# Gate weight sums kept in DRAM, head 0's data and the first token sums loaded from an earlier place, and the pools of branch A moved, in a hybrid attention encoder block

## The chip, the cores and the metric

One Trainium2 chip, of which the kernel uses one core. The metric is the device time of one execution in microseconds (us), lower is better. The engines are called as the profile calls them: PE (TensorE matmuls) with PEld (its weight loads), DVE (VectorE), ACT (ScalarE), POOL (GpSimd) and SP (SyncE, which issues every DMA of this kernel from one queue, in order).

## The reference

One encoder block on 1024 tokens of width 1024, in float32, with 16 meta tokens in front. Two attention branches share one input projection; each branch is projected back to width 1024, multiplied by a sigmoid gate, and the two are added; then comes an output projection and a SwiGLU feed-forward part.

```python
proj = h @ w_in                       # qa, ka, va, qb, kb, vb, ga, gb
y_a = differential_attention(qa, ka, va, ...)   # 4 heads, two softmax maps each, all keys
y_b = windowed_gqa(qb, kb, vb, sink)            # 8 heads, 128-wide window
merged = sigmoid(ga) * (y_a @ w_ba) + sigmoid(gb) * (y_b @ w_bb)
h = h + merged @ w_o
h = h + (silu(n(h) @ w_gate) * (n(h) @ w_up)) @ w_down
return rms_norm(h)[:, 16:]
```

In differential attention a head's weights are `softmax(s1) - lambda * softmax(s2)`; each score matrix is one "map" m of the kernel.

## The kernel before

**Precision.** Every large matrix product is made of three float32r products: an operand is split into a high half (a copy by ACT, line 114) and a low half (a subtraction, line 115, on POOL or DVE), and high x high, high x low and low x high are added in PSUM. `split` is this helper, so a split operand costs one ACT and one POOL or DVE instruction whatever line calls it.

**Stages.** Input norm and transposition; projections, with branch B's attention (`units_b`) run between those of branch A's heads (`project_a`, lines 561 to 573); then branch A's attention, into whose PE order the gate products are woven (lines 823 to 866); then the merge (lines 901 to 974), the output projection, and the feed-forward part. Projected queries, keys and values of branch A go to DRAM (`qa_d`, `ka_d`, `va_d`) and come back a head at a time by `load_a(h)` (line 704).

**The gates** are two 1024 x 1024 products, made with a Strassen-like scheme of 7 products instead of 8 for each of 8 column blocks k: 56 products (p, k) in the order `order_g` (lines 603 to 609), each of 4 steps of 3 matmuls (`gate_steps`, line 667), together 672 matmuls with 512 columns. Product 2, 1 and 4 use a block of `w_in` as it is. Products 5, 3, 6 and 7 need sums of blocks: a21+a22 (s1), s1-a11 (s2), a12-s2 (s4), a11-a21 (s3). `g_prep` (line 622) loads the raw blocks of w_in (`gr`), makes the sums in place on POOL (lines 644 to 650, four for each k, 32 in all), and splits the operand (`gop`). For products 5 and 3 it makes s1, s2 and s4 and puts s2 away in DRAM (`s2_d`); for product 1 it loads the raw blocks again. It runs three products ahead of PE. The other operand is the transposed normed input hT or a token sum; `load_sums` (line 596) overwrites parts of hT with token sums from DRAM when their readers are done. A finished product goes to DRAM (`g_d`), and products 1, 6 and 7 add what lies there (`gk`).

**Branch A's loop** (lines 831 to 859) runs over 4 heads x 8 query tiles, one tile at a time. PE's order is written out by hand: SLOTS is a string with one letter for each action of a tile, s for a chunk of scores (6 for a tile), g for one gate step, t for a transposition of the tile before, n for a step of the values and their norm. At the first tile of a head come G_FIRST (head 0) or G_HEAD gate steps; 36 steps are held back for the end. A tile's chain is: scores on PE, bias and minimum on DVE (line 737), exponential on ACT (742), scaling of map 1 on POOL (745), combination on DVE (748), a copy of the last 16 columns on POOL (749), transposes on PE (760), splits into `at` on ACT and DVE (763, 764), values on PE (773).

**What sets the order.** PE's order in branch A is manual. All other orders, and PE's order among the projections, come from a scheduler that places instructions by a simulated timeline when the kernel is built; on the chip each engine and SP's queue then run theirs strictly in order. Pools are stacks from the left and from the right of the on-chip memory: a pool opened after another was closed takes its addresses, and the first write to a tile waits for the last use of what lay there. In before, `bpool` (left, branch B's tiles) stays open until after the projections; then `gpool` (right) and `apool` (left) are opened.

Of the kernel before, what the change touches and what calls it, by code (L numbers as in the profile page):

```python
# [19 lines left out]
P = 128  # L20
# [19 lines left out]
SLOTS = "sgsgsngsgsstntnt"  # L40
S_BUFS = (2, 2)
AT_BUFS = 2
G_BUFS = 3
GV_BUFS = 4
# [4 lines left out]
G_FIRST = 30  # L49
# [21 lines left out]
def encoder_block(ctx: ExitStack, tc: tile.TileContext, x, meta, norm_mix, w_in, lq1, lk1, lq2, lk2,  # L71
# [30 lines left out]
    s2_d = [dram.tile([P, 4, P], F32, name=f"s2_d{k}") for k in range(8)]  # L102
# [124 lines left out]
    def project_v(col, name, evac):  # L227
        vt = bpool.tile([P, L + NM], F32, tag="vt", name=f"vt_{name}", bufs=1)
        project(col, K_CHUNKS, name, lambda ps, at, n: nc.scalar.copy(vt[:, at:at + n], ps))
        nc.vector.tensor_copy(vt[:, L:L + NM], vt[:, S:L])  # L230

        def turn():
            for b in range(3):
                nb = 4 if b < 2 else 1
                kp = P if b < 2 else 2 * NM
                pt = pp_bank(f"pv_{name}_{b}").rearrange("p (c t) -> p c t", c=4)
                for i in range(nb):
                    k = 4 * b + i
                    nc.tensor.transpose(pt[:kp, i, :], vt[:, k * P:k * P + kp], ident)
                evac(pt[:kp, :nb, :], 4 * b, nb, kp)  # L240
                yield

        turning_v[:] = [turn()]
# [6 lines left out]

    bpool, close_bpool = pool("bpool")
# [121 lines left out]
    def norm_x(t):  # L373
        parts = P if t < NT else NM
        i = len(done)
        done.append(t)
        tag, bufs = ("vt", 1) if i % 3 == 2 else ("bs", 2)
        xns[t] = normed(bpool, xts.pop(t)[:parts], parts, gmix, f"a{t}", tag=tag, bufs=bufs)
# [182 lines left out]
    units_b(0, qb, first_b)  # L561
# [9 lines left out]
    project_a(2)  # L571
    project_a(3)
    flush_v()
    close_bpool()
    close_psum1()


    def branch_w(p, o, src, nme, raw=None):
        w = (raw_tile(f"wbr{nme}_{o}")[:, 0:512] if raw is None else raw).rearrange("p (c n) -> p c n", n=P)
        nc.sync.dma_start(w, src[:, o * P:(o + 1) * P].rearrange("(c p) n -> p c n", p=P))  # L580
        wh = p.tile([P, 2, 4, P], F32R, tag="wh", name=f"wbh{nme}_{o}", bufs=WB_BUFS)
        split(wh[:, 0], wh[:, 1], w, nc.gpsimd)
        return wh

    def branch_mm(ps, w, src, tk):
        for j in range(4):
            for n, (a, b) in enumerate(((0, 0), (0, 1), (1, 0))):
                nc.tensor.matmul(ps, w[:, a, j, :], src(j, b, tk),  # L588
                                 start=(j == 0 and n == 0), stop=(j == 3 and n == 2))

    close_tpool()
    close_stage()
    close_wpool()
    gpool, close_gpool = pool("gpool", "right")
# [5 lines left out]
    load_sums(5, 0, 1)  # L600
# [11 lines left out]
    def g_cols(k):  # L612
        return (C_GB, C_GA)[k // 4] + k % 4 * 256

    def g_tile(name):
        return gpool.tile([P, 512], F32, tag="gv", name=name, bufs=GV_BUFS)

# [4 lines left out]
    def g_prep(n):  # L622
        p, k = order_g[n]
        at, tt = g_cols(k), nc.gpsimd.tensor_tensor

        def load(out, kh, c0, cn):
            nc.sync.dma_start(out, w_in[kh * 512:kh * 512 + 512, at + c0:at + c0 + cn].rearrange("(c p) n -> p c n", p=P))

        if p == 2:
            src = g_tile(f"g12_{k}").rearrange("p (c n) -> p c n", n=P)  # L630
            load(src, 1, 0, P)
        else:
            if p in (5, 1):
                raw = g_raw[k] = gpool.tile([P, 2, 4, 256], F32, tag="gr", name=f"gr{p}_{k}", bufs=2)
                load(raw[:, 0], 0, 0, 256)
                if p == 5:
                    load(raw[:, 1], 1, 0, 256)
                else:
                    nc.sync.dma_start(raw[:, 1, :, 0:P], s2_d[k])
                    load(raw[:, 1, :, P:256], 1, P, P)  # L640
            raw = g_raw[k]
            a11, a21, a12, a22 = (raw[:, i, :, j * P:j * P + P] for i in range(2) for j in range(2))
            if p == 5:
                tt(a21, a21, a22, ALU.add)
            elif p == 3:
                tt(a11, a21, a11, ALU.subtract)
                nc.sync.dma_start(s2_d[k], a11)
                tt(a12, a12, a11, ALU.subtract)
            elif p == 7:
                tt(a21, a11, a21, ALU.subtract)  # L650
            src = {5: a21, 3: a12, 1: a11, 6: a12, 7: a21, 4: a22}[p]
            if p in (1, 6, 7):
                kept = g_kept[p, k] = g_tile(f"gk{p}_{k}")
                nc.sync.dma_start(kept, g_place(p, k))
        op = g_ready[p, k] = gpool.tile([P, 2, 4, P], F32R, tag="gop", name=f"gop{p}_{k}", bufs=4)
        split(op[:, 0], op[:, 1], src, nc.gpsimd)

    g_prepped = [0]

    def g_ahead(n):  # L660
        while g_prepped[0] < min(n, len(order_g)):
            g_prep(g_prepped[0])
            g_prepped[0] += 1

    g_ahead(3)

    def gate_steps():
        for n, (p, k) in enumerate(order_g):
            g_ahead(n + 3)
            op, act = g_ready.pop((p, k)), G_ACT[p]  # L670
            if p in (2, 5, 1):
                g_bank[k] = pp_bank(f"pg{p}_{k}")
            ps = g_bank[k]
            for c in range(4):
                for i, (a, b) in enumerate(((0, 0), (0, 1), (1, 0))):
                    nc.tensor.matmul(ps, op[:, a, c], quad(b, *act)[:, c], start=(p in (2, 5, 1) and c == 0 and i == 0),  # L676
                                     stop=(p in (2, 3, 4) and c == 3 and i == 2), skip_group_check=True)
                if c == 3:
                    if p in (1, 6, 7):
                        st = g_kept.pop((p, k))  # L680
                        nc.vector.tensor_tensor(st, ps, st, ALU.add)
                    else:
                        st = gpool.tile([P, 512], F32, tag="g", name="gate_stage", bufs=G_BUFS)
                        nc.scalar.copy(st, ps)
                    nc.sync.dma_start(g_place(p, k), st)
                    if k == 7 and p in (2, 5, 3):
                        load_sums({2: 6, 5: 7, 3: 4}[p], *act)
                yield

    apool, close_apool = pool("apool")  # L690
    psum2, close_psum2 = pool("psum2", space=PSUM)
    psum1 = psum2
# [27 lines left out]

    def scores_a(h, t, ld, s):
# [6 lines left out]
        for m in (1, 0):  # L728
            s[m] = s0s[t % 2] if m == 0 else apool.tile([P, L], F32, tag="s1", name=f"as1_{nm}", bufs=S_BUFS[1])
# [19 lines left out]
        nc.gpsimd.tensor_copy(s[0][:, L:L + 2 * NM].rearrange("p (a k) -> p a k", a=2),  # L749
# [27 lines left out]
    def normed_a(h, c, py):  # L777
        nm = f"{h}_{c}"
        ysq = apool.tile([P, 512], F32, tag="ysq", name=f"ysq_{nm}", bufs=1)
        nc.scalar.activation(ysq, py, AF.Square)  # L780
        yg = apool.tile([P, 512], F32, tag="yg", name=f"yg_{nm}", bufs=2)
        nc.scalar.activation(yg, py, AF.Copy, scale=gsub)
        yield
        pst = bank(psum2, "sc", f"apst_{nm}", SC)
        for i in range(4):
            nc.tensor.matmul(pst[:, i:i + 1], ysq[:, i * P:(i + 1) * P], ones, start=True, stop=True)
        f = small.tile([P, 4], F32, tag="af", name=f"af_{nm}", bufs=2)
        nc.vector.tensor_scalar(f, pst[:, 0:4], 1.0 / P, EPS, ALU.mult, ALU.add)
        nc.gpsimd.tensor_tensor(f, f, neg_half, ALU.pow)
        for _ in range(N_WAIT):  # L790
            yield
        pf = bank(psum2, "sc", f"apf_{nm}", SC)
        for i in range(4):
            nc.tensor.transpose(pf[:, i * P:(i + 1) * P], f[:, i:i + 1].broadcast_to([P, P]), ident)
# [36 lines left out]
    for n in range(AH * NT + T_LAG):  # L831
        scoring, turning = iter(()), iter(())
        if n < AH * NT:
            h, t = divmod(n, NT)
            if t == 0:
                ld = load_a(h)
                fill(G_HEAD if h else G_FIRST)
            if t % 2 == 0:
                at_ = apool.tile([P, 9, 2, 256], F32R, tag="at", name=f"at{h}_{t}", bufs=AT_BUFS)
# [5 lines left out]
        for what in SLOTS:  # L845
# [18 lines left out]
    order_pe.__exit__(None, None, None)  # L864
    close_apool()
    fill(1000)
# [570 lines left out]
```

## Time and profile before

| What | us |
|---|---|
| median of 3 runs | 1504.69 |
| the three runs | 1504.47, 1504.69, 1507.2 |
| the profiled execution | 1502.53 |
| its span in the profile | 1500.8 |

The stages lie in the profile about like this (from the chain of waits and the stretches):

| Stage | from, to (us from the span's start) |
|---|---|
| input norm, projections, branch B | 0 to 307 |
| branch A with the gate products | 307 to 665 |
| merge | 674 to 763 |
| output projection | 763 to 888 |
| feed-forward and output | 888 to 1501 |

Times are us unless marked ns. A row of stretches gives start:end, length, busy time and number of instructions of each engine, the clock that PE was granted as a share of full speed, the mean busy share of the 16 DMA engines, and GB/s. In rows of groups the pair after the bar is busy time and mean ns of one. In rows of waits come the total, the number of times and the longest. "a<-b" is the tile written and the tile read, and L with a number the line of the kernel.

### The profile page before, as it was taken

The numbers are of one execution on the slowest core, as the hardware profiler recorded it, in microseconds if no ns is written. First come the engines' busy times: TensorE is split into PE (matmuls) and PEld (weight loads), VectorE is DVE, ScalarE is ACT, GpSimd is POOL, SyncE is SP. The second block draws the span as 40 slices with busy tenths as digits, with TensorE's granted clock in tenths as the row PEclk, the third lists the DMA queues.
The fourth block names the chain that finished last, engine by engine and source line by source line (L and its number), as shares of the span: only waits on it lengthen the run. The fifth ranks groups of instructions, "written<-read, shape, count | busy, mean of one in ns | idle before, by whom it ended". The sixth has DMA issues, their size and how long they took to land.

```text
span 1500.8 us, 21142 instructions
## 1 busy us (share of the span) xinstructions
PE 1434.8 (96%) x7279; PEld 1227.3 (82%) x7279; DVE 884.2 (59%) x1578; ACT 680.3 (45%) x1293; POOL 674.6 (45%) x622
## 2 busy tenths in 40 slices
PE   8999999947999999979999999999999999999997
PEld 7998989936888898868888878888888888788886
DVE  7477436503867797823440786655555554778666
ACT  6366436513655465534521563433333333344444
POOL 4599233318646454423732476554544453000344
PEclk9999999978999999989999999999999999999999
DMA  8467442297386836466740345333333333864443
GB/s 239 98 188 234 127 114 83 62 276 224 105 283 218 258 123 199 133 226 180 212 161 21 135 119 161 106 106 105 106 105 106 106 105 105 288 238 133 128 125 140
DMA packets 184570, 231.92 MB, mean 155 GB/s; under 512 B 17984, under 2 KB 115712, under 8 KB 184464
## 3 DMA queue, kind: packets, MB, share of 16 engines
q1 hardware_dynamic: 184464, 230.58, 49.2%
q8 instruction: 57, 0.93, 0.3%
q14 instruction: 49, 0.40, 0.1%
HBM read 153.26 MB, written 70.71 MB: 149 GB/s over the span
## 4 chain that ended last, share of the span: by engine, by line
PE 68%; DMA 10%; POOL 9%; issue 5%; DVE 5%; ACT 2%; SPq 1%; POOLq 0%; DVEq 0%; ACTq 0%
PE pg L1218 26%; PE pd L1312 8%; PE po L995 5%; PE pg L676 5%; PE ppa L588 4%; DMA gr<-in_w_in_dram 4%; PE pp_qb L201 3%; POOL oa L115 3%; PE aps L734 2%; PE pp_va L201 2%; DMA ak<-ka_d 2%; PE pp_qa L201 2%; PE apy L773 2%; PE pp_ka L201 2%; PE bpt L339 1%
## 5 line engine op out<-in xcount | busy, mean ns | idle before, releaser
L115 POOL TENSOR_TENSOR wop<-wf,wop 128x512 fp32r<-128x512 f32 x128 | 172.5, 1352 | 166.3 <-ACT wop L114 150.3
L1218 PE MATMUL pg<-t,wop 128*128 128x512 f32 x1056 | 242.6, 389 | 0.0
L1218 PEld LDWEIGHTS pg<-t,wop 128*128 128x128 f32 x1056 | 198.3, 188 | 41.1
L1312 PE MATMUL pd<-ob,oa 128*128 128x512 f32 x924 | 210.2, 389 | 1.8 <-DVE ob L115 1.4
L1312 PEld LDWEIGHTS pd<-ob,oa 128*128 128x128 f32 x924 | 173.3, 188 | 38.6 <-DVE ob L115 1.8
L676 PE MATMUL pg<-hT_hi,gop 128*128 128x512 f32 x448 | 168.7, 408 | 20.8 <-ACT gop L114 19.6
L1218 PE MATMUL pg<-b,wop 128*128 128x512 f32 x792 | 185.6, 392 | 2.9 <-DVE c L1227 2.9
L1218 PEld LDWEIGHTS pg<-b,wop 128*128 128x128 f32 x792 | 149.5, 189 | 34.8 <-issue 2.4
L115 POOL TENSOR_TENSOR oa<-ra,oa 128x512 fp32r<-128x512 f32 x33 | 44.0, 1335 | 171.8 <-ACT oa L114 170.4
L676 PEld LDWEIGHTS pg<-hT_hi,gop 128*128 128x128 f32 x448 | 87.0, 195 | 38.1 <-ACT gop L114 20.8
L114 ACT ACTIVATE wop<-wf 128x512 fp32r<-128x512 f32 x128 | 80.2, 631 | 83.7 <-PE pg L1218 48.5
L114 ACT ACTIVATE oa<-ra 128x512 fp32r<-128x512 f32 x77 | 48.6, 632 | 107.6 <-PE pd L1312 48.9
L734 PE MATMUL aps<-ak,aq 128*128 128x392 f32 (+1 forms) x384 | 91.2, 332 | 3.8 <-DVE amn L737 2.2
L742 ACT ACTIVATE as<-as,amn 128x1040 f32<-128x1040 f32 x64 | 74.5, 1164 | 43.4 <-DVE amn L737 39.6
L676 PE MATMUL pg<-hT_lo,gop 128*128 128x512 f32 x224 | 90.8, 405 | 0.0
L1053 DVE TENSOR_TENSOR s<-wf,wf 128x512 f32<-128x512 f32 x22 | 27.0, 1228 | 104.5 <-DMA wf<-in_w_ff_gate_dram 56.6
L995 PE MATMUL po<-woh,mT 128*128 128x512 f32 x384 | 88.0, 390 | 0.0
L115 POOL TENSOR_TENSOR gop<-gr,gop 128x512 fp32r<-128x512 f32 x48 | 66.9, 1396 | 41.0 <-ACT gop L114 37.9
L734 PEld LDWEIGHTS aps<-ak,aq 128*128 128x128 f32 x384 | 70.9, 192 | 17.6 <-DVE amn L737 3.5
L995 PEld LDWEIGHTS po<-woh,mT 128*128 128x128 f32 x384 | 71.9, 188 | 14.8
L737 DVE CUSTOM_DVE_ANT_0 as<-aps,dist,far_a 128x392 f32<-128x392 f32 x64 | 39.5, 618 | 62.8 <-PE aps L734 62.4
L326 POOL TENSOR_SCALAR bs<-bs,bdn 128x432 f32<-128x432 f32 (+1 forms) x64 | 39.4, 634 | 60.6 <-DVE bdn L324 52.5
(275 smaller groups left out, 3075.1 us busy)
## 6 DMA issues: line engine op xcount, KB each, us to landing
ra<-aop SPq DMA_DIRECT2D x77, 256.0 KB, 2.7
gr<-in_w_in_dram SPq DMA_DIRECT2D x24, 512.0 KB, 5.7
wf<-in_w_ff_gate_dram SPq DMA_DIRECT2D x24, 512.0 KB, 3.8
wf<-in_w_ff_up_dram SPq DMA_DIRECT2D x24, 512.0 KB, 3.8
aop<-as SPq DMA_DIRECT2D x44, 256.0 KB, 2.1
w_c<-in_w_in_dram SPq DMA_DIRECT2D x17, 512.0 KB, 5.0
aop<-c SPq DMA_DIRECT2D x33, 256.0 KB, 2.0
ts_d<-to SPq DMA_DIRECT2D x16, 512.0 KB, 3.8
```

Of the source, the lines that this page charges most:

```text
L114: nc.scalar.activation(hi, src, AF.Copy)
L115: lo_eng.tensor_tensor(lo, src, f32(hi), ALU.subtract)
L201: nc.tensor.matmul(ps[:, :n], a[:, c, :], b[:, c, at:at + n], start=(c == 0 and i == 0), stop=(c == DC - 1 and i == 2))
L326: nc.gpsimd.tensor_scalar(st[:, r, :W], st[:, r, :W], dn[:, r:r + 1], 1.0, ALU.mult, ALU.mult)
L588: nc.tensor.matmul(ps, w[:, a, j, :], src(j, b, tk), start=(j == 0 and n == 0), stop=(j == 3 and n == 2))
L676: nc.tensor.matmul(ps, op[:, a, c], quad(b, *act)[:, c], start=(p in (2, 5, 1) and c == 0 and i == 0), stop=(p in (2, 3, 4) and c == 3 and ...
L734: nc.tensor.matmul(ps[:, :n], qs[m][:, t * P:(t + 1) * P], ks[m][:, vv, k0:k0 + n], start=(vv == 0), stop=(vv == 1))
L737: nc.vector.tensor_tensor_reduce(s[m][:, k0:k0 + n], ps[:, :n], far_by, slope, low, ALU.add, ALU.min, mn[:, m, i:i + 1])
L742: nc.scalar.activation(s[m][:, 0:L], s[m][:, 0:L], AF.Exp, bias=low, scale=-1.0, accum_out=dn[:, m:m + 1])
L995: nc.tensor.matmul(ps, mT[:, c, a, t * P:(t + 1) * P], wos[q, c][:, b], start=(c == 0 and n == 0), stop=(c == DC - 1 and n == 2))
L1218: nc.tensor.matmul(ps, op[:, x, c, :], b[:, y, c, :], start=(p in (1, 2, 5) and c == 0 and n == 0), stop=(p in (4, 2, 3) and c == 3 and n ...
L1312: nc.tensor.matmul(ps[u], oa[:, a, u * P:(u + 1) * P], ob[:, b, :], start=(p in (1, 2, 5) and j == 0 and k == 0), stop=(p in (2, 3, 4) and ...
```

## The change

- `bpool` is closed as soon as branch B's second group has been written down in the program, before `project_a(2)`. `apool` is opened there, with head 0's tiles, the two score buffers of map 0 and the masked distances, and `load_a(0)` is called there. The transposed values (`vt`) get a pool of their own (`vtpool`), since `project_a` still needs them.
- A new pool `wspool` is opened next, and `weight_sums` makes the 32 sums with POOL from raw blocks `gw` (16 loads of 512 KB, 2 buffers), k = 0 to 3 after `project_a(2)` and k = 4 to 7 after `project_a(3)`, and stores them in DRAM (`ws_d`, 32 stores of 256 KB, 6 buffers). `s2_d` is gone.
- Each gate product then loads just its own operand of 256 KB (`g_load`, up to 5 products ahead) and splits it (`g_split`, up to 3 ahead). The first two operands are loaded into and split in the weight buffers of the projections (`w_g`, `w_gop`). `load_sums(5, 0, 1)` stands before `flush_v()`.
- `gpool` has smaller and other buffers (6 of 2 KB for loads, 4 of 4 KB, 3 of 2 KB, 2 of 2 KB). The map 1 scores, `at`, `ysq` and `yg` move into a pool `apool2`, opened after `wspool` is closed.
- The copy of line 749 goes from POOL to DVE.
- G_FIRST goes from 30 to 4, and SLOTS has five gate steps a tile for the first 24 tiles (SLOTS_LAST, with four as before, for the last 8).

```diff
-SLOTS = "sgsgsngsgsstntnt"
+SLOTS = "sgsgsngsgsgstntnt"
+SLOTS_LAST = "sgsgsngsgsstntnt"
...
-G_BUFS = 3
-GV_BUFS = 4
+G_BUFS = 2
+GK_BUFS = 3
+GR_BUFS = 6
+GO_BUFS = 4
...
-G_FIRST = 30
+G_FIRST = 4
...
+    def weight_sums(k, p):
+        tt = nc.gpsimd.tensor_tensor
+        raw = p.tile([P, 2, 4, 256], F32, tag="raw", name=f"gw_{k}", bufs=2)
+        for kh in range(2):
+            nc.sync.dma_start(raw[:, kh], g_weights(k, kh, 0, 256))
+        a11, a21, a12, a22 = (raw[:, i, :, j * P:j * P + P] for i in range(2) for j in range(2))
+        s1, s2, s3, s4 = (p.tile([P, 4, P], F32, tag="sum", name=f"gs{i}_{k}", bufs=6) for i in range(4))
+        tt(s1, a21, a22, ALU.add)
+        tt(s2, s1, a11, ALU.subtract)
+        tt(s4, a12, s2, ALU.subtract)
+        tt(s3, a11, a21, ALU.subtract)
+        for i, t in ((5, s1), (3, s4), (6, s2), (7, s3)):
+            nc.sync.dma_start(ws_d[i, k], t)
...
+    def g_load(n, raw=None):
+        p, k = order_g[n]
+        if raw is None:
+            raw = gpool.tile([P, 512], F32, tag="gr", name=f"gr{p}_{k}", bufs=GR_BUFS)
+        raw = raw.rearrange("p (c n) -> p c n", n=P)
+        nc.sync.dma_start(raw, ws_d[p, k] if (p, k) in ws_d else g_weights(k, *{2: (1, 0), 1: (0, 0), 4: (1, P)}[p], P))
+        g_raw[p, k] = raw
+
+    def g_split(n, op=None):
+        p, k = order_g[n]
+        if op is None:
+            op = gpool.tile([P, 2, 4, P], F32R, tag="gop", name=f"gop{p}_{k}", bufs=GO_BUFS)
+        split(op[:, 0], op[:, 1], g_raw.pop((p, k)), nc.gpsimd)
+        g_ready[p, k] = op
+        if p in (1, 6, 7):
+            kept = g_kept[p, k] = gpool.tile([P, 512], F32, tag="gk", name=f"gk{p}_{k}", bufs=GK_BUFS)
+            nc.sync.dma_start(kept, g_place(p, k))
...
     units_b(1, qb)
+    close_bpool()
+    apool, close_apool = pool("apool")
...
+    ld = load_a(0)
+    wspool, close_wspool = pool("wspool")
     project_a(2)
+    for k in range(4):
+        weight_sums(k, wspool)
     project_a(3)
+    for k in range(4, 8):
+        weight_sums(k, wspool)
+    for n in range(2):
+        g_load(n, wpool.tile([P, DC, P], F32, tag="w", name=f"w_g{n}", bufs=2)[:, 0:4].rearrange("p c n -> p (c n)"))
+        g_split(n, wpool.tile([P, DC, P], F32R, tag=("wh", "wl")[n], name=f"w_gop{n}", bufs=W_BUFS)
+                .rearrange("p (a c) n -> p a c n", a=2))
+    g_done[:] = [2, 2]
+    load_sums(5, 0, 1)
     flush_v()
-    close_bpool()
     close_psum1()
+    close_wspool()
...
+    gpool, close_gpool = pool("gpool", "right")
+    g_ahead(0)
+    psum2, close_psum2 = pool("psum2", space=PSUM)
+    psum1 = psum2
+    apool2, close_apool2 = pool("apool2")
...
-            s[m] = s0s[t % 2] if m == 0 else apool.tile([P, L], F32, tag="s1", name=f"as1_{nm}", bufs=S_BUFS[1])
+            s[m] = s0s[t % 2] if m == 0 else apool2.tile([P, L], F32, tag="s1", name=f"as1_{nm}", bufs=S_BUFS[1])
...
-        nc.gpsimd.tensor_copy(s[0][:, L:L + 2 * NM].rearrange("p (a k) -> p a k", a=2),
+        nc.vector.tensor_copy(s[0][:, L:L + 2 * NM].rearrange("p (a k) -> p a k", a=2),
...
-                ld = load_a(h)
+                if h:
+                    ld = load_a(h)
...
-        for what in SLOTS:
+        for what in SLOTS if n < 3 * NT else SLOTS_LAST:
```

More of the change, by code (lines that the diff above doesn't have):

```diff
@@ L101, in encoder_block @@
     ts_d = {p: dram.tile([P, 2, 4, 512], F32, name=f"ts_d{p}") for p in (5, 6, 7, 4)}
-    s2_d = [dram.tile([P, 4, P], F32, name=f"s2_d{k}") for k in range(8)]
+    ws_d = {(p, k): dram.tile([P, 4, P], F32, name=f"ws_d{p}_{k}") for p in (5, 3, 6, 7) for k in range(8)}
     ya_d = [dram.tile([P, S], F32, name=f"ya_d{h}") for h in range(4)]
@@ L559, in units_b, with load_sums @@
             p()
+    def load_sums(p, kh, half):
+        for hl in range(2):
+            nc.sync.dma_start(f32(quad(hl, kh, half)), ts_d[p][:, hl])
+    G_ACT = {2: (1, 0), 5: (0, 1), 3: (1, 1), 1: (0, 0), 6: (1, 0), 7: (0, 1), 4: (1, 1)}
+    G_OUT = {2: (0, 0), 5: (1, 1), 3: (0, 1), 1: (0, 0), 6: (0, 1), 7: (1, 1), 4: (1, 0)}
+    order_g = [(2, k) for k in range(4)]
+    for k in range(0, 8, 2):
+        order_g += [(p, k + i) for p in (5, 3) for i in range(2)]
+        if k < 4:
+            order_g += [(2, k + 4 + i) for i in range(2)]
@@ new lines, in g_place @@
+    def g_place(p, k):
+        row, half = G_OUT[p]
+        return g_d[2 * k + row][:, half * 512:half * 512 + 512]
+    def g_load(n, raw=None):
[14 more added lines that the diff above has]
+            nc.sync.dma_start(kept, g_place(p, k))
@@ L561, in encoder_block, with g_ahead @@
+    g_done = [0, 0]
+    def g_ahead(n):
+        for i, (what, far) in enumerate(((g_load, GR_BUFS - 1), (g_split, GO_BUFS - 1))):
+            while g_done[i] < min(n + far, len(order_g)):
+                what(g_done[i])
+                g_done[i] += 1
     units_b(0, qb, first_b)
@@ L585, in branch_mm @@
[L585 to L594, printed above, removed]
-    def load_sums(p, kh, half):
-        for hl in range(2):
-            nc.sync.dma_start(f32(quad(hl, kh, half)), ts_d[p][:, hl])
@@ L610, in encoder_block @@
-    g_ready, g_raw, g_kept, g_bank = {}, {}, {}, {}
[L612 to L616, printed above, removed]
-    def g_place(p, k):
-        row, half = G_OUT[p]
-        return g_d[2 * k + row][:, half * 512:half * 512 + 512]
[L622 to L688, printed above, removed]
@@ new lines, in branch_mm, with gate_steps @@
+    def branch_mm(ps, w, src, tk):
+        for j in range(4):
+            for n, (a, b) in enumerate(((0, 0), (0, 1), (1, 0))):
+                nc.tensor.matmul(ps, w[:, a, j, :], src(j, b, tk),
+                                 start=(j == 0 and n == 0), stop=(j == 3 and n == 2))
+    def gate_steps():
+        for n, (p, k) in enumerate(order_g):
+            g_ahead(n + 1)
+            op, act = g_ready.pop((p, k)), G_ACT[p]
+            if p in (2, 5, 1):
+                g_bank[k] = pp_bank(f"pg{p}_{k}")
+            ps = g_bank[k]
+            for c in range(4):
+                for i, (a, b) in enumerate(((0, 0), (0, 1), (1, 0))):
+                    nc.tensor.matmul(ps, op[:, a, c], quad(b, *act)[:, c], start=(p in (2, 5, 1) and c == 0 and i == 0),
+                                     stop=(p in (2, 3, 4) and c == 3 and i == 2), skip_group_check=True)
+                if c == 3:
+                    if p in (1, 6, 7):
+                        st = g_kept.pop((p, k))
+                        nc.vector.tensor_tensor(st, ps, st, ALU.add)
+                    else:
+                        st = gpool.tile([P, 512], F32, tag="g", name="gate_stage", bufs=G_BUFS)
+                        nc.scalar.copy(st, ps)
+                    nc.sync.dma_start(g_place(p, k), st)
+                    if k == 7 and p in (2, 5, 3):
+                        load_sums({2: 6, 5: 7, 3: 4}[p], *act)
+                yield
```

56 lines of the change are left out of this document (28 added, 28 removed).

## The prediction

> **What bounds the kernel now.** I read the page first, then the busy time by stretch, TensorE's waits, and the chain of waits at both ends of branch A.
>
> ```profile
> PE 1434.8 (96%) x7279; PEld 1227.3 (82%) x7279; DVE 884.2 (59%) x1578; ACT 680.3 (45%) x1293; POOL 674.6 (45%) x622
> ...
> 306.74:673.54 366.80, 320.51 (x1842) 282.81 (x1841) 225.10 (x619) 182.85 (x340) 177.23 (x165) 0.94 0.64 202
> 306.74:322.30 15.56, 0.00 (x1) 0.00 (x1) 0.56 (x1) 1.12 (x2) 0.00 (x0) 0.56 0.96 259
> 322.30:354.30 32.00, 26.74 (x90) 19.47 (x91) 0.00 (x0) 9.02 (x16) 19.05 (x16) 0.84 0.99 290
> 417.70:490.00 72.30, 67.60 (x405) 60.93 (x403) 51.24 (x147) 41.05 (x80) 38.77 (x36) 0.95 0.79 256
> 490.00:664.90 174.90, 170.85 (x1035) 153.11 (x1033) 123.87 (x338) 90.14 (x168) 77.01 (x77) 1.00 0.56 177
> 664.90:673.54 8.64, 0.20 (x2) 0.00 (x1) 1.18 (x2) 6.22 (x10) 0.00 (x0) 0.63 1.05 405
> ```
>
> Columns: stretch and length, then busy time of PE, PEld, DVE, ACT, POOL, granted clock, DMA share, GB/s. TensorE is the bound of the whole kernel, and the change touches only what lies between the last projection (306.74) and the first merge product (673.54). In these 366.80 us PE is busy 320.51; the idle time sits at the two ends and in the first heads, while from 490 to 664.9 PE is idle only 4.05 of 174.90 us (2.3%).
>
> ```profile
> PE pg L676 <- ACT gop L114: 19.6, 3, 15.6
> PE apt L760 <- DVE as L748: 8.8, 4, 4.5
> PE ppa L588 <- ACT yb L114: 8.4, 1, 8.4
> PE apt L760 <- POOL as L749: 4.3, 2, 2.7
> ...
> 306.81 5.25 DMA hT_hi<-ts_d
> ...
> 316.17 9.61 DMA ak<-ka_d
> 325.80 12.77 DMA gr<-in_w_in_dram
> ...
> 642.03 0.82 PE apy L773 x7
> 642.86 4.21 PE pg L676 x18
> 647.06 0.78 PE apst L786 x8
> ...
> 654.22 0.44 PE apf L794 x4
> ...
> 660.66 7.05 DMA tb<-yb_d
> 667.77 5.05 DMA g_d<-gate_stage
> ```
>
> The first lines are PE's waits (total, times, longest), the others the chain (start, length). The first gate product waits 15.6 us because its weights queue behind head 0's keys. The chain also gives the rate of full work: 4.21/18 = 0.234 us a gate matmul, 0.82/7 = 0.117 a value matmul, 0.44/4 = 0.11 a transpose, 0.78/8 = 0.098 for L786. A score matmul comes from PE's timeline:
>
> ```profile
> 354.31 0.51 PE L734 MATMUL aps<-ak,aq 128*128 128x392 f32 x2
> 354.65 0.39 PE L676 MATMUL pg<-hT_hi,gop 128*128 128x512 f32 x1
> ...
> 356.39 0.40 PE L734 MATMUL aps<-ak,aq 128*128 128x256 f32 x2
> 356.63 0.40 PE L676 MATMUL pg<-hT_hi,gop 128*128 128x512 f32 x1
> ```
>
> From start to start two take 0.34 us (392 wide) or 0.24 (256 wide), so a tile's scores (two maps of 2 + 2 + 2) take 2 x (0.34 + 0.34 + 0.24) = 1.84. How often each occurs, by stretch for L676 (gates), L734 (scores, 32 tiles), L760 (transposes), L773 (values), L786 and L794, with busy time and count:
>
> ```profile
> 306.74:673.54 366.80, 186.59 (x672) 0.94 0.64 202
> 306.74:673.54 366.80, 91.22 (x384) 0.94 0.64 202
> 306.74:673.54 366.80, 46.15 (x288) 0.94 0.64 202
> 306.74:673.54 366.80, 58.06 (x400) 0.94 0.64 202
> 306.74:673.54 366.80, 7.60 (x64) 0.94 0.64 202
> 306.74:673.54 366.80, 4.80 (x32) 0.94 0.64 202
> ```
>
> At the full rates that is 157.2 + 58.9 + 31.7 + 46.8 + 6.3 + 3.5 = 304.4 us of work: 62.4 of the 366.8 are lost to waits and a lowered clock, and that is all there is to win.
>
> **The change part by part.** The order in which the changed program's instructions stand on each engine decides it, and it is not what the words say. The new pool of the weight sums takes addresses of branch B's pool (its transposes and exponentials), and branch B's second group runs among the last projections until the end. So on SP the first load of a weight sum stands behind the last key store and head 0's whole load; on POOL all 32 sums stand behind branch B's last scaling, and **ahead of the first scaling of a head-0 tile** (L745). PE's order is written out: 4 gate steps, tile 0's scores, 5 steps, tile 1's scores with 5 steps, then tile 0's transposes. Those need L748's result, which needs L745's, which stands behind the last sum. PE therefore stops after 14 steps (42 matmuls) and two tiles: 42 x 0.234 + 2 x 1.84 = 13.5 us of work. (It pauses once before, as the third gate product's low half stands on POOL behind the first five sums; that lies inside the longer wait.)
>
> *When the last sum is done.* It is a matter of bytes in one queue. From head 0's load to the last weight load SP issues: head 0, 4152 KB (queries 2 x 512, keys 2 x 1040, values 1024, and 24); 16 weight loads of 512; 24 stores of sums of 256; 10 gate-weight loads of 256; 4 gate moves of 256. Sum 22,072 KB = 22.6 MB.
>
> ```profile
> 311.06 0.60 SPq L710 DMA_DIRECT2D aq<-qa_d  x1
> ...
> gr<-in_w_in_dram SPq DMA_DIRECT2D x24, 512.0 KB, 5.7
> ...
> L646 POOL TENSOR_TENSOR gr<-gr 128x512 f32<-128x512 f32 x8 | 10.3, 1285 | 0.3
> ...
> L745 POOL TENSOR_SCALAR as<-as,adn,neglam 128x1040 f32<-128x1040 f32 x32 | 38.9, 1215 | 36.4 <-DVE adn L743 33.7 <-DVE af L788 2.7
> ...
> L749 POOL COPY as<-as 128x32 f32<-128x32 f32 x32 | 7.7, 240 | 30.5 <-DVE as L748 30.5
> ...
> L748 DVE SCALAR_TENSOR_TENSOR as<-as,adn,as x32: 1280/1301/2446, 365.9 to 632.1; 128x1040 f32<-128x1040 f32 x32
> ```
>
> Head 0's load issues at 311.06 as now (SP's order ahead of it is nearly the same), and the queue is free at 312.1 (306.81 + 5.25). A full queue moved 290 GB/s (share 0.99), at best 256/0.79 = 324, at worst 259/0.96 = 270. At 290 the bytes take 78 us, to 390; the last four sums add 4 x 1.285 = 5.1: **395**. At 324: 387; at 270: 401. I take 290, whose stretch has the same mix of loads. The Trainium skill's "DMA: Bandwidth & Descriptors", Specifications, puts the HBM limit of one core at about 358 GB/s; by that the bytes would need 63 us, an estimate, and the last sum would end at 380, 15 us earlier in the sum; the row of 290 GB/s at share 0.99 doesn't reach it, though other stretches come nearer.
>
> POOL's own floor: the first pair of weights can land at 328 (5.3 MB at 324 GB/s from 312), then 32 sums and 4 gate splits of the same shape make 36 x 1.285 = 46.3: 375. Above, if loads become a chain: only two raw buffers, so each load is issued after the sums two before it; with a landing of 12.8 us as in the full queue at 325.80, a weight takes (12.8 + 5.1)/2 = 9 us, and six from about 350 end near 404, plus 5: 409.
>
> After the last sum come L745 (1.2) and L748 (1.3 alone, up to 2.4; I take 2.3, POOL being busy beside it): PE resumes at 395 + 3.5 = **398.5**, with 304.4 - 13.5 = 290.9 us still to do.
>
> *Restart.* After the 15.6 us gap:
>
> ```profile
> 322.30 0.79 PE L676 MATMUL pg<-hT_hi,gop 128*128 128x512 f32 x1 [15.56 <-ACT gop L114]
> ...
> 326.14 0.64 PE L676 MATMUL pg<-hT_hi,gop 128*128 128x512 f32 x2
> ```
>
> Eight matmuls took 3.84 us instead of 1.9, so a cold start costs 2; I take 3, since tile 1's chain is late too (bounds 2 and 5). The Trainium skill's "TensorE: Matmul & The Clock Gate", Part 1, says half clock for about 3.4 us after an idle window; that would be 1.7 us lost, an estimate, and the sum 1 us less; the 3.84 us row agrees roughly.
>
> *The rest of branch A.* Nothing else is on POOL's path there: 32 sums are gone from it, and L749 (one 128x32 copy a tile) is DVE's. Its price on DVE is not shown; between 0 and 32 x 0.24 = 7.7 us, hidden, as DVE is busy 123.87 of 174.90 us. Of the 4.3 + 8.8 us that PE waited for L749 and L748 some part returns. The fifth gate slot for 24 tiles replaces the first fill (30 steps to 4): 186 steps for 188, no PE work changed. Gate weights now come as 256 KB loads five products ahead, so the first heads should run like today's late ones: 2.3% of 270 us = 6 us lost (bounds 2 and 10).
>
> *Merge.* The branch B splits (yb) no longer wait for the last gate store (667.77 + 5.05) and stand ahead of the sigmoids on ACT. They then follow the load of tb, 660.66 + 7.05 = 667.7, against gates ending at 664.9: I take a gap of 4 (bounds 0 and the 8.6 of now). Two gate weights, split beside the projections, add 2 x 1.4 us to POOL and let 8 steps start at once; they lie inside the wait.
>
> *Sum.* 398.5 + 290.9 + 3 + 6 + 4 = 702.4 against 673.54: **+28.9 us**. On the profiled execution's 1502.53 that is 1531.4; the median of the runs, 1504.69, is 2.2 above it, so runs would lie at 1531 to 1534. I say 1532. As a check on the middle, the gate matmuls (L676) that are done by 396 now:
>
> ```profile
> 306.74:396.00 89.26, 45.13 (x150) 0.81 0.75 223
> ```
>
> 150 against 42: the change is 25 us behind there in gates alone.
>
> **The rivals.**
> *It does what it says* (not slower). The sums run beside the last projections, where POOL and the queue have room:
>
> ```profile
> 250.00:298.00 48.00, 48.00 (x299) 43.81 (x297) 26.73 (x62) 24.92 (x58) 18.32 (x34) 1.00 0.23 61
> ```
>
> (POOL 18.32 of 48 us, DMA share 0.23.) PE then only waits for head 0's keys, from 309.6 (after 4 steps) to about 318 (1.57 MB from 312 at 270 GB/s). End: 306.74 + 304.4 + 8.4 + 13 = 632.5, 41 us less: 1461. It decides if POOL's last sum is done before tile 0's exponentials, near 355. Against it: the order, and 375 as the earliest end. Chance 0.05.
> *POOL's floor* (almost no change). Loads keep ahead, the last sum ends at 375; 375 + 2.5 + 290.9 + 2 + 4 + 4 = 678.4, +5: 1507. For it: 5.7 us a load and 324 GB/s later; against it: 290 with head 0's load in front. Chance 0.09, a third of it within 0.2%.
> *Loads in a chain* (slower still). Last sum at 409, merge as late as now: 412.5 + 290.9 + 5 + 10 + 8.6 = 727, +53.5: 1556. For it: 12.77 us in a full queue. Chance 0.12.
>
> **How the numbers follow.** The forecast has 0.74; its own range, with the sum's end at 387 to 401 and the small terms' bounds, is 1519 to 1545. The range asked for takes in half of each slower or equal neighbour: 1509 to 1552. Faster by over 0.2% (3 us, about what a measurement of this kernel tells from no change) 0.05; within 0.2% 0.03; slower 0.92.
>
> **What would show it.** PE idle from about 346 to 398 with the wait put down to L748 or POOL; the first L745 right behind the last sum, near 395; DMA share near 1 from 312 to 390; no POOL sums after it; a merge gap of 4 us. It is wrong if the sums stand in the trace before 306, if they end before 375, or if PE idles more than 10 us between 400 and the merge.

## The result, and the profile after

| | kernel before | changed kernel |
|---|---|---|
| median of the runs (us) | 1505.95 (4 runs, 1504.47 to 1508.0) | 1522.44 (4 runs, 1521.53 to 1524.26) |
| the profiled execution, its span (us) | 1502.53, 1500.8 | 1522.86, 1521.1 |
| first merge product (us from the span's start) | 673.54 | 691.29 |

The changed kernel is **slower**: ratio 1.011, 95% interval 1.0093 to 1.0128, or 16.5 us between the medians (20.3 between the profiled executions). The forecast was 1532 us.

The windows of the changed kernel (columns as in the prediction: stretch, length, busy PE, PEld, DVE, ACT, POOL, clock, DMA share, GB/s):

```profile
306.61:391.80 85.19, 20.07 (x69) 15.29 (x68) 9.12 (x28) 8.73 (x15) 47.33 (x38) 0.61 0.95 315
...
312.00:330.00 18.00, 7.73 (x22) 5.88 (x22) 0.63 (x2) 0.10 (x1) 0.00 (x0) 0.62 1.01 282
320.00:340.00 20.00, 9.17 (x24) 6.39 (x24) 1.27 (x4) 1.85 (x3) 6.19 (x5) 0.59 1.03 323
340.00:360.00 20.00, 7.78 (x30) 6.65 (x30) 4.95 (x20) 5.81 (x10) 18.48 (x16) 0.67 1.02 347
360.00:380.00 20.00, 0.00 (x0) 0.00 (x0) 0.00 (x0) 0.00 (x0) 14.21 (x13) 0.50 1.04 367
...
391.80:520.00 128.20, 128.20 (x765) 116.34 (x766) 98.74 (x283) 79.31 (x152) 51.99 (x41) 0.98 0.53 176
520.00:691.29 171.29, 167.94 (x1010) 150.31 (x1008) 121.78 (x341) 86.91 (x163) 64.81 (x53) 1.00 0.55 183
```

In the first 85 us of branch A PE works 20. From 391.80 it never rests until 520, and it rests 3.35 us from there to the first merge product. From 312 to 380 the DMA engines are full (share above 1). POOL is nearly full from 340 to 360 (18.48 of 20 us), but not from 360 to 380 (14.21): there the sums wait for their weights.

PE's waits, then its timeline and POOL's around the long one (start, length, operation; in brackets the idle time ahead of it and what ended it):

```profile
PE apt L771 <- DVE as L759: 43.4, 2, 42.7
PE aps L745 <- DMA ak<-ka_d: 13.9, 4, 10.5
PE pg L718 <- ACT gop L117: 7.7, 1, 7.7
PE pg L718 <- POOL gop L118: 2.2, 1, 2.2
...
348.69 0.40 PE L745 MATMUL aps<-ak,aq 128*128 128x256 f32 x2
391.80 2.18 PE L771 MATMUL apt<-ident,as 128*128 128x128 f32 x9 [42.70 <-DVE as L759]
```

```profile
333.65 1.26 POOL L592 TENSOR_TENSOR gs<-gw 128x512 f32<-128x512 f32 x1 [37.40 <-DMA gw<-in_w_in_dram]
...
383.06 1.26 POOL L592 TENSOR_TENSOR gs<-gw 128x512 f32<-128x512 f32 x1 [2.04 <-issue]
384.40 1.26 POOL L593 TENSOR_TENSOR gs<-gs,gw 128x512 f32<-128x512 f32 x1
385.74 1.26 POOL L594 TENSOR_TENSOR gs<-gw,gs 128x512 f32<-128x512 f32 x1
386.96 1.26 POOL L595 TENSOR_TENSOR gs<-gw 128x512 f32<-128x512 f32 x1
388.21 1.20 POOL L756 TENSOR_SCALAR as<-as,adn,neglam 128x1040 f32<-128x1040 f32 x1
```

The rows show the order: the first scaling of a head-0 tile (L756, L745 before) starts at 388.21, the instant the last sum ends. DVE's combination follows, and PE's transposes at 391.80.

### The profile page after: what moved, and what is told of

Read it like the earlier page. It is cut to its first block, busy times and chain, and to the rows that moved or that the text cites. A ratio compares the mean times of both kernels' runs of the same rounds, so it can differ in the third digit from the quotient of the medians.

```text
span 1521.1 us, 21195 instructions
## 1 busy us (share of the span) xinstructions
PE 1433.7 (94%) x7279; PEld 1227.9 (81%) x7279; DVE 888.8 (58%) x1610; ACT 679.3 (45%) x1293; POOL 663.1 (44%) x590
## 4 chain that ended last, share of the span: by engine, by line
PE 72%; DMA 8%; POOL 8%; issue 5%; DVE 3%; ACT 2%; SPq 0%; POOLq 0%; DVEq 0%; ACTq 0%
PE pg L1232 25%; PE pd L1326 8%; PE pg L718 7%; PE po L1009 5%; PE ppa L706 4%; PE aps L745 3%; PE pp_qb L204 3%; PE apy L784 3%; POOL oa L118 3%; PE pp_va L204 2%; PE apt L771 2%; DMA gw<-in_w_in_dram 2%; PE pp_qa L204 2%; PE pp_ka L204 2%; DMA ak<-ka_d 1%
## 5 line engine op out<-in xcount | busy, mean ns | idle before, releaser
L718 PE MATMUL pg<-hT_hi,gop 128*128 128x512 f32 x432 | 162.7, 399 | 9.9 <-ACT gop L117 7.7
L118 POOL TENSOR_TENSOR gop<-gr,gop 128x512 fp32r<-128x512 f32 x54 | 74.5, 1380 | 121.2 <-ACT gop L117 115.3
L745 PE MATMUL aps<-ak,aq 128*128 128x392 f32 (+1 forms) x384 | 96.2, 335 | 13.9 <-DMA ak<-ka_d 13.9
L718 PEld LDWEIGHTS pg<-hT_hi,gop 128*128 128x128 f32 x432 | 82.3, 190 | 22.8 <-ACT gop L117 8.0
L745 PEld LDWEIGHTS aps<-ak,aq 128*128 128x128 f32 x384 | 72.1, 195 | 29.9 <-issue 13.8
L771 PE MATMUL apt<-ident,as 128*128 128x128 f32 x288 | 45.3, 279 | 43.7 <-DVE as L759 43.4
L718 PE MATMUL pg<-hT_lo,gop 128*128 128x512 f32 x216 | 86.1, 398 | 0.0
L1067 DVE TENSOR_TENSOR s<-wf,wf 128x512 f32<-128x512 f32 x22 | 18.8, 856 | 106.6 <-DMA wf<-in_w_ff_gate_dram 55.0
L771 PEld LDWEIGHTS apt<-ident,as 128*128 128x128 f32 x288 | 34.3, 145 | 44.5 <-DVE as L759 43.8
```

Of the source, the lines that this page charges most:

```text
L118: lo_eng.tensor_tensor(lo, src, f32(hi), ALU.subtract)
L745: nc.tensor.matmul(ps[:, :n], qs[m][:, t * P:(t + 1) * P], ks[m][:, vv, k0:k0 + n], start=(vv == 0), stop=(vv == 1))
L771: nc.tensor.transpose(pt[:kp, j, :], s[:, k * P:k * P + kp], ident)
```

## The experiments

All are edits of the changed kernel, and each expectation was written before its run. Where one time is given, it is that of one execution. The runs come from several chips, on which the kernel before took 1503.96 to 1506.7 us (medians).

### The sums at other addresses

```diff
-        raw = p.tile([P, 2, 4, 256], F32, tag="raw", name=f"gw_{k}", bufs=2)
+        raw = [p.tile([P, 4, 256], F32, tag="to", name=f"gw{kh}_{k}", bufs=2) for kh in range(2)]
...
-        s1, s2, s3, s4 = (p.tile([P, 4, P], F32, tag="sum", name=f"gs{i}_{k}", bufs=6) for i in range(4))
+        s1, s2, s4 = (p.tile([P, 4, P], F32, tag="ta", name=f"gs{i}_{k}", bufs=3) for i in (0, 1, 3))
...
+        nc.sync.dma_start(ws_d[5, k], s1)
+        s3 = p.tile([P, 4, P], F32, tag="ta", name=f"gs2_{k}", bufs=3)
...
-    wspool, close_wspool = pool("wspool")
...
-        weight_sums(k, wspool)
+        weight_sums(k, tpool)
```

> The weight sums get the addresses of the token sums' pool (free since about 152 us) in place of branch B's; nothing else changes but their buffers (one pair of raw halves, three sums). Theory (the late sums are a matter of addresses): all 32 sums stand in the trace between 150 and 306 us, none after; PE waits at the start of branch A only for head 0's keys (about 10 us) and then runs through; the first merge product starts near 306.7 + 304.4 + 13 + 9 = 633 us and the run takes 633 + 831.6 (what follows the first merge product in the changed kernel) = 1465 us, 1455 to 1480. Rival A (the sums only move their cost: POOL and the queue disturb the projections): the last projection ends after 315 us and the run takes over 1490. Rival B (too few gate steps at the start and five a tile are what costs): projections as now, but PE idles over 25 us between 307 and 400, over 1495.

**1477.78 us** (4 runs; ratio to the kernel before 0.9823, interval 0.9796 to 0.9851), and 1477.37 (0.9821, 0.9807 to 0.9835) when it ran again as the base of the last experiment:

> The kernel of the first run again, on the same chip and in the same rounds as the last one, as the base for it: 1475 to 1480 us, 0.982 of the kernel before.

The sums' instructions (count, shortest, median and longest ns, first and last start), PE's waits, and two windows of this kernel:

```profile
L592 POOL TENSOR_TENSOR gs<-gw,gw x8: 1284/1294/1296, 160.6 to 268.4; 128x512 f32<-128x512 f32 x8
...
L597 POOL TENSOR_TENSOR gs<-gw x8: 1284/1290/1309, 164.5 to 274.7; 128x512 f32<-128x512 f32 x8
...
PE aps L745 <- DMA ak<-ka_d: 11.7, 4, 8.9
PE bps L318 <- DMA qb<-qk_stage: 3.8, 1, 3.8
PE pg L718 <- ACT gop L117: 3.6, 1, 3.6
...
200.00:250.00 50.00, 44.86 (x241) 39.57 (x241) 24.79 (x60) 23.79 (x58) 29.94 (x30) 0.97 0.78 225
...
317.30:350.00 32.70, 18.78 (x63) 14.68 (x63) 8.19 (x26) 8.05 (x14) 6.51 (x6) 0.69 0.94 295
```

The same sums, in the same place of the program and with fewer buffers, now run from 160.6 to 276, and the long wait is gone: the addresses held them back. The time lies in the theory's range, but 13 us above its middle, because rival A was right in part. The first gate product starts at 317.11 and not at 306.78, 10.3 us later: between 200 and 250 us PE is idle for 5.14 us and does 241 products (293 in the changed kernel). Its longest wait there, 3.8 us, is for branch B's queries; in the queue's order their transfers stand behind two loads of raw weights, which is argued from that order and not tested by a run of its own.

### The first scalings on DVE

```diff
-                (nc.gpsimd if t % 4 in COMBINE_POOL else nc.vector).tensor_scalar(
+                (nc.gpsimd if (h, t) > (0, 1) else nc.vector).tensor_scalar(
```

> The scalings of map 1 of head 0's first two tiles go from POOL to DVE, so that they no longer stand behind the sums in POOL's order. If that order alone holds PE (the prediction's step), PE resumes near 355 in place of 391.8 and the run takes about 1488 us. If the addresses hold a second lock (the transposed weights' buffer lies where the raw blocks lie), tile 0's transposes come near 355, but PE stops again within two score chunks and two gate steps, for the split into that buffer, until the last sums and their stores are done near 393: 1520 to 1526 us, no gain.

1513.87 us, between the two. PE's timeline, then ACT's:

```profile
355.94 2.18 PE L771 MATMUL apt<-ident,as 128*128 128x128 f32 x9 [7.43 <-DVE as L759]
389.45 0.80 PE L745 MATMUL aps<-ak,aq 128*128 128x256 f32 x2 [27.58 <-DVE at L775]
...
388.07 1.08 ACT L774 ACTIVATE at<-apt 128x512 fp32r<-128x512 f32 x2 [34.17 <-DMA ws_d<-gs]
```

The transposes come at 355.94, as expected, and PE stops again for the split into `at`. Its addresses were those of the sums' pool, and ACT's wait of 34.17 us for it is put down to the store of a sum. So there are two locks (instructions that hold PE) with one key, the end of the sums. My price of the second was too high: it opens at 388, without the scaling and the combination behind it, so that PE goes on at 389.45 in place of 391.80; and PE had already worked 5.93 us from 355.94 on, at a granted clock of 0.52, about 3 us at full speed.

### Half of the stores left out, and three raw buffers

In the first kernel only the sums of products 5 and 3 are stored; the second has `bufs=3` for `gw` in addition.

```diff
-        for i, t in ((5, s1), (3, s4), (6, s2), (7, s3)):
+        for i, t in ((5, s1), (3, s4)):
...
+        nc.sync.dma_start(raw, ws_d[p, k] if p in (5, 3) else g_weights(k, *{2: (1, 0), 1: (0, 0), 4: (1, P), 6: (0, 0), 7: (0, P)}[p], P))
```

> The sums of products 6 and 7 are made but not stored (16 of 32 stores), and those products take plain blocks of the same size, so their results differ. About 12 of the left-out stores, 3.1 MB, stood ahead of the last weight load. Theory (bytes in one queue set the last sum): at 355 GB/s it ends 9 us earlier, near 379, and the run takes about 1513 us. Rival (POOL's own time): the last sum ends at 388 as now, 1522 us. Rival (a chain of loads behind two raw buffers): at most 2 us earlier, 1520 us.

> As the run without half of the stores (products 6 and 7 take plain blocks, so their results differ), and three raw buffers in place of two. There the last sum ended at 384.0, 4.2 us earlier, where bytes alone gave 9. If the loads are then a chain behind two buffers, the last sum now ends at 380 or earlier, which is POOL's floor (332.7 + 36 x 1.26 = 378), and the run takes about 1512 us; if POOL's waits have another cause it stays at 384 and 1516 us.

1516.59 us, between the theory's time and that of the chain, and 1513.61 us. The window that was fullest before, in the first kernel, and the last sum in the second:

```profile
360.00:380.00 20.00, 0.00 (x0) 0.00 (x0) 0.00 (x0) 0.00 (x0) 16.14 (x13) 0.50 0.82 278
```

```profile
372.73 1.26 POOL L595 TENSOR_TENSOR gs<-gw 128x512 f32<-128x512 f32 x1
377.85 1.26 POOL L595 TENSOR_TENSOR gs<-gw 128x512 f32<-128x512 f32 x1
379.11 1.20 POOL L756 TENSOR_SCALAR as<-as,adn,neglam 128x1040 f32<-128x1040 f32 x1
```

With fewer bytes the last sum ended at 384.0, not at the 379 of bytes alone: the queue is no longer full (0.82), and two buffers chain the loads. With a third buffer POOL runs four sums each 5.12 us without a gap and ends at 379.1, its floor. So the three limits of the prediction lie within 9 us of each other: the sums end at 388 with all the stores, at 384 by the chain, at 379 by POOL.

The chain is at work in the changed kernel too. There each of the last six pairs of raw loads was issued 0.4 to 1.2 us after the sum that freed its buffer, the last pair like this:

```profile
372.73 1.26 POOL L595 TENSOR_TENSOR gs<-gw 128x512 f32<-128x512 f32 x1
...
374.39 1.41 SPq L589 DMA_DIRECT2D gw<-in_w_in_dram  x2
```

Three buffers with all the stores were not run, so how much of the 9 us is bytes and how much is the chain stays open.

### The sums on DVE

```diff
-        tt = nc.gpsimd.tensor_tensor
+        tt = nc.vector.tensor_tensor
```

> The changed kernel with its 32 sums on DVE in place of POOL, same place, same buffers. Theory (bytes in one queue): the last weights land near 383 as now, the last sum ends near 386, PE resumes near 390 and the run takes 1519 to 1523 us. Rival (POOL's time, of which 36 instructions of 1.26 us from 333.65 to 388.2 fill 45 of 54.6 us, holds the loads back through the two raw buffers): the last weights land before 377, PE resumes before 383, under 1515 us.

1519.68 us. One window, DVE's first sum and two of its last:

```profile
360.00:380.00 20.00, 0.00 (x0) 0.00 (x0) 8.09 (x12) 0.00 (x0) 0.00 (x0) 0.50 1.07 387
...
336.80 0.69 DVE L592 TENSOR_TENSOR gs<-gw 128x512 f32<-128x512 f32 x1 [2.65 <-DMA gw<-in_w_in_dram]
...
381.95 0.69 DVE L592 TENSOR_TENSOR gs<-gw 128x512 f32<-128x512 f32 x1 [2.81 <-issue]
384.01 0.68 DVE L595 TENSOR_TENSOR gs<-gw 128x512 f32<-128x512 f32 x1
```

Each sum takes 0.69 us in place of 1.26, and still the last weights are there only 1.1 us earlier (381.95 against 383.06), not before 377 as the rival had it. In the changed kernel the queue is the main limit of the last sum, as in the theory, but not the only one. Here the first sum started 3.1 us later (336.80 against 333.65), so from the first weights to the last it took 45.2 us in place of 49.4, and from 360 to 380 the queue moved 387 GB/s in place of 367. The difference of about 4 us, in one execution of each, is best put down to POOL's slower sums, which free the two raw buffers later.

### More gate steps first

```diff
-G_FIRST = 4
+G_FIRST = 28
...
-        for what in SLOTS if n < 3 * NT else SLOTS_LAST:
+        for what in SLOTS_LAST:
```

> 28 gate steps ahead of head 0's first scores and four a tile throughout, in place of 4 and five; the sums stay where they are. Theory (the sums end by the queue whatever PE does, so PE work ahead of the wait is a pure gain): 22 more steps of 0.70 us are done before the wait, 15 us; the last sum comes up to 4 us later, since five more operand loads of 256 KB stand ahead; the idle time at tile 0's transposes falls from 42.7 to about 30 us and the run takes 1508 to 1512 us. Rival (the operands of those steps come from the stored sums and wait on POOL and SP behind the rest): under 5 us gained, over 1517.

1518.32 us: the rival's gain of under 5 us, over 1517 as it said. PE's waits, ACT's longest, and POOL at the end of the sums:

```profile
PE pg L718 <- ACT gop L117: 28.8, 1, 28.8
PE apt L771 <- DVE as L759: 24.9, 2, 24.3
...
341.85 1.33 ACT L117 ACTIVATE gop<-gr 128x512 fp32r<-128x512 f32 x2 [27.52 <-DMA gr<-in_w_in_dram]
...
396.76 1.26 POOL L595 TENSOR_TENSOR gs<-gw 128x512 f32<-128x512 f32 x1
```

The wait is split in two, no more. The first part is for an operand that is a plain block of the weights, and not a stored sum, which the rival had named: its load stands in the queue behind head 0's data and the first raw weights. The last sum ends at 398.0, 10 us later. Cover did not help here, since its own data stood in the same queue.

### The merge's gap

```diff
-GK_BUFS = 3
+GK_BUFS = 5
...
+    for i in range(3):
+        gpool.tile([P, 512], F32, tag="gk", name=f"gk_skip{i}", bufs=GK_BUFS)
```

> The changed kernel with two more buffers for the kept gate halves, which lie lowest in the gate pool and reach 3 KB into the addresses of the last branch B operand (yb3). In the built order its splits then stand behind the sigmoids of the gates on ACT again, as in the kernel before. Theory (the merge's gap is ACT's order behind the loads of the last gates): the gap ahead of the first merge product grows from 1.0 to 6 to 9 us and the run by the same, 1528 to 1531 us. Rival (the gap is set by the load of branch B's output alone): gap 1 to 2 us, 1522 to 1524 us.

1528.16 us. The wait of PE in the changed kernel, then in this one, and this one's timeline of ACT:

```profile
PE ppa L706 <- ACT yb L117: 1.0, 1, 1.0
...
PE ppa L708 <- ACT yb L117: 8.7, 1, 8.7
...
690.79 0.59 ACT L728 COPY gate_stage<-pg 128x512 f32<-128x512 f32 x1 [2.20 <-PE pg L720]
691.40 1.28 ACT L952 ACT_TABLE_LOAD   x1
694.36 1.92 ACT L952 ACTIVATE gt<-gt 128x512 f32<-128x512 f32 x3 [1.68 <-DMA gt<-g_d]
...
698.80 4.26 ACT L117 ACTIVATE yb<-tb 128x512 fp32r<-128x512 f32 x8
```

A few KB of overlap put the splits of branch B's output (yb) behind the sigmoids, and the wait is back at 8.7 us. The wait grows by 7.7 us and the profiled execution by 5.3 (1522.86 to 1528.16), since the merge itself went faster here (90.7 us against 94.0). So the smaller gate pool is worth 5 to 8 us; the theory's "by the same" holds for the wait alone.

### What is left at the start of branch A

Both kernels have the sums at the token sums' addresses and 16 gate steps first. The first loads the third and fourth gate operand early into the same addresses; the second the third to seventh, and it has three stage buffers. The first has five load buffers and the second four, in place of six. The diff is that of the second, without the lines shown above.

```diff
-G_BUFS = 2
+G_BUFS = 3
-GR_BUFS = 6
+GR_BUFS = 4
-G_FIRST = 4
+G_FIRST = 16
...
+    for n in range(2, 5):
+        g_load(n, tpool.tile([P, 512], F32, tag="ta", name=f"t_g{n}", bufs=3))
+    for n in range(5, 7):
+        g_load(n, tpool.tile([P, 2, 512], F32, tag="to", name=f"t_g{n}", bufs=2)[:, 0])
+    g_done[:] = [7, 2]
...
-        for what in SLOTS if n < 3 * NT else SLOTS_LAST:
+        for what in SLOTS if n < 12 else SLOTS_LAST:
```

> The sums at the token sums' addresses, as before in this study, and in addition 16 gate steps in place of 4 ahead of head 0's first scores (five a tile for the first 12 tiles only), with the raw operands of the third and fourth gate product loaded early into the same addresses. Theory (what is left at the start of branch A is PE without work while head 0's keys come): 12 steps of 0.70 us, 8.4 us, fill the wait of about 10 us, and the wait of 3.6 us for the third operand goes; 1477.8 - 8 to 12 = 1466 to 1470 us. Rival (the steps only move the wait: operands or token sums for the next products are late instead): under 3 us gained, over 1475.

> As the run with 16 gate steps first, but the raw operands of the third to seventh gate product all come early into the token sums' addresses, and there are three gate stage buffers in place of two (four operand loads in flight in place of five). There PE lost 9.7 us to the copy of a finished gate product, which stood on ACT behind the split of an operand that came behind head 0's loads. Theory (that order held PE): the wait falls under 3 us, PE runs on gate steps until head 0's keys land, and the run takes 1477.8 - 8 to 13 = 1465 to 1470 us. Rival (the store of a finished product, also behind head 0's loads, holds the stage buffers and PE in the same way): a wait over 5 us put down to the gate stage stays, and the run takes 1472 to 1476 us.

The first took 1474.93 us (4 runs; ratio 0.9798, interval 0.9777 to 0.9818), under 3 us less than without the steps: its rival was right, and the gain is not clear of noise, since the intervals overlap. PE, then ACT, in that kernel:

```profile
341.33 0.80 PE L720 MATMUL pg<-hT_hi,gop 128*128 128x512 f32 x1 [9.74 <-ACT gate_stage L728]
...
340.02 0.63 ACT L117 ACTIVATE gop<-gr 128x512 fp32r<-128x512 f32 x1 [18.72 <-DMA gr<-ws_d]
340.69 0.59 ACT L728 COPY gate_stage<-pg 128x512 f32<-128x512 f32 x1
```

ACT stands 18.72 us at the split of an operand that comes behind head 0's loads, and the copy that would free PE's bank stands behind it. The second kernel took **1470.15 us** (6 runs; ratio 0.9786, interval 0.9761 to 0.9812), against 1477.37 for its base on the same chip, and has the lowest median of this study. Its waits at that place:

```profile
PE aps L749 <- DMA ak<-ka_d: 3.5, 3, 2.0
PE pg L722 <- ACT gate_stage L730: 2.0, 1, 2.0
```

The wait fell from 9.7 to 2.0 us, as in the theory, whose range of times the median just misses, and in the profiled executions the first merge product came at 638.0 against 650.0 in the base. But the six runs spread from 1466.38 to 1480.98 us and the base's four from 1474.1 to 1479.51, so the 7 us between the medians are not clear of noise. Whether the earlier operands or the third stage buffer took the wait away, no run tells apart.

## Why the prediction was right, and which terms were off

**The mechanism held.** The sums stand ahead of the first scaling on POOL, the wait is put down to the chain behind L756 and L759, the queue is full until 380, no sum comes later, and 14 gate steps and two tiles are what PE did first (42 gate and 24 score matmuls). Moving the sums to free addresses takes the wait away. But the prediction named one lock of two: the run with the first scalings on DVE shows that `at`'s addresses alone would have held PE until 389.45. Both open with the last sum, so the forecast time hardly depends on it. The small pause for the third gate product lies inside the longer wait, as said, but only 2.2 us of it are the low half on POOL, as the prediction had it; 7.7 us are the high half on ACT, which waits for its load. PE's wait for head 0's keys (13.9 us), which the sum left out, lies inside it too.

**The terms of the sum**, on the profiled executions (the merge was forecast for 702.4 and began at 691.29, 11.1 us earlier):

| Term | forecast | measured | difference |
|---|---|---|---|
| end of the last sum | 395 | 388.2 | -6.8 |
| scaling and combination | 3.5 | 3.6 | +0.1 |
| PE work left | 290.9 | 294.0 | +3.1 |
| restart | 3 | 2.2 | -0.8 |
| rest of branch A | 6 | 2.3 | -3.7 |
| merge's gap | 4 | 1.0 | -3.0 |
| after the first merge product | 0 | 2.5 | +2.5 |

The work left is what remains of 299.5 us (391.80 to 691.29) after the other three. The counts are those of the forecast (630 gate matmuls and 360 of scores were left), so its 3.1 us, 1%, lie in the rates or in pauses too short to show. The rest of branch A is the 3.35 us of idle time after 520 less the gap. The 2.5 us are the difference of the two profiled executions (20.3) less that of the merge's starts (17.75). All in all 20.3 and not 28.9; the medians differ by 4 us less, since the profiled execution of before was 3.4 us under its median and that of the changed kernel 0.4 above. The four terms that were too high add up to 14.3 us and the three that were too low to 5.7, so the mechanism was right, but part of the nearness is luck.

- **The end of the last sum** is the term that was mis-sized most. I divided 22.6 MB by one rate, 290 GB/s, from a stretch of the kernel before. The queue moved 282 GB/s from 312 to 330, and then 323, 347 and 367 in the three windows above. From 312.6, when the token sums had landed, to 383.06 the 22.6 MB make 321 GB/s, near my upper bound of 324, which gave 387. That bound itself was not the best rate in the rows of the prediction: from 664.90 to 673.54 the kernel before moved 405 GB/s, at share 1.05. The Trainium skill's "DMA: Bandwidth & Descriptors", Specifications, gives about 358 GB/s, by which I worked out 380, an estimate: 8.2 us too early, where my 395 was 6.8 too late. The trace has 357 as the mean from 340 to 380, which agrees, but 367 from 360 to 380 and 309 from 312 to 340; why the first part is slower at the same share, no run shows. The tail of four sums (383.06 to 388.2, forecast 5.1) was right.
- **The rivals.** POOL's floor was given as 375 and is 379.1, since the first weights came at 333.4 in that run and not at 328. The chain of loads exists, at 384 with half the stores, not 409: a load of the changed kernel lands in 6.9 us (median), not 12.8. "It does what it says" was put at 1461 us; with the sums really beside the projections it is 1477.8. That sum left out the 10.3 us that the projections then lose, and took the wait for head 0's keys as 8.4 us, where the run shows 11.7.
- **Restart.** The clock's rows after the long wait:

```profile
391.80:393.80 2.00, 2.00 (x10) 2.00 (x11) 1.36 (x4) 1.56 (x3) 1.21 (x1) 0.50 0.38 115
393.80:395.80 2.00, 2.00 (x7) 1.71 (x7) 1.13 (x4) 0.83 (x3) 0.00 (x0) 0.50 0.00 0
395.80:397.80 2.00, 2.00 (x11) 1.78 (x10) 2.00 (x5) 0.61 (x2) 0.00 (x0) 0.90 0.00 0
```

Two windows at half clock and one at 0.90 lose 2.2 us. By the Trainium skill's "TensorE: Matmul & The Clock Gate", Part 1, it would have been 1.7, an estimate; the rows show about 4 us at half clock, a little more than its 3.4.

- **The rest of branch A and the gap.** The rest was taken at the rate of loss of the kernel before, 2.3%. But with POOL free of sums, the copy on DVE and the operands loaded further ahead, PE ran 128 us without a pause; which of these did it, no run tells apart. The gap became 1.0 because branch B's splits stand ahead of the sigmoids on ACT; the run with that order undone shows 8.7.

What stays open: the 2.5 us after the first merge product. The merge took 94.0 us here, against 89.6 in the kernel before and 90.5 to 93.7 in the runs above, and what follows took 1.9 us less than in the kernel before. In the merge PE waits 2.3 us for a weight split, which the other runs show at 0.3 to 1.8 or not at all; it may be that one execution, and no run was made for it.

## What to carry to other kernels

Where work is moved "beside" a busy stage, look at what lies under its buffers: a pool that takes the addresses of a live pool moves its first load, and everything behind it on in-order engines, to the end of that pool's life. Before adding cover, ask which queue the cover's own data stands in. When a wait is a matter of bytes in a queue, bound it by several rates, and work out the buffers' chain and the engine's floor beside it, since they may lie only a few us apart and act together.

## What the runs showed of the hardware that was not expected

- 387 GB/s over 20 us for one core (share 1.07), with loads of 512 KB and stores of 256 KB mixed, in the kernel with the sums on DVE; 367 in the changed kernel (share 1.04). At a share of 1.01 the changed kernel also moved only 282 (312 to 330), so a full share doesn't tell the rate.
- A sum of 128x512 took 0.69 us on DVE and 1.26 us on POOL while the other engines were idle, and 1.29 us on POOL beside the projections.
